# A hybrid convolution and attention layer: which converted weights are kept in DRAM, marks per group of values, and the meta tokens' values by head

## The chip, the core and the metric

The kernel runs on one core of a Trainium2 chip. The time is that of one execution on the device, in microseconds (us). Of several executions the median counts. A profile comes from one execution, and its span runs from the first to the last instruction.

The engines named below each take their instructions in order: TensorE (PE) multiplies matrices and transposes, with its weight loads as PEld; VectorE (DVE) and ScalarE (ACT) do arithmetic on what PE leaves in its accumulators and on buffers; GpSimd (POOL) does arithmetic on buffers and starts some transfers from its own DMA queue (q0); SyncE (SP) starts the other transfers (q1). Sixteen DMA engines move the data of both queues.

## What is computed

One layer over 2048 frames of 1024 channels, with 16 learned meta tokens ahead of them. Both halves of the layer read one input projection of the normalized input:

```python
u = rms_norm(h, pre_g)
proj = u @ w_in
glu_a, glu_b, conv_gate, q, k, v, sb_gate = split(proj)      # 7 x 512 columns

c = glu_a * sigmoid(glu_b)
c = causal_depthwise_conv(c, conv_w, conv_b)                  # width 31
c = silu(layer_norm(c, conv_ln_g, conv_ln_b))
c = c @ w_pw2 + b_pw2                                         # second convolution product
c = c * silu(conv_gate)

s = stick_breaking_attention(q, k, v)                         # 8 heads x 64, strictly causal
s = s * silu(sb_gate)

mixed = concatenate([c, s]) @ w_out
h = h + rms_norm(mixed, post_g)                               # the meta tokens are dropped
```

In the stick-breaking attention the weight of key s for query t is beta(t, s) times the product of 1 - beta(t, j) over the keys j between them, with beta = sigmoid(q.k / 8). The kernel forms the running products P with a scan from the last key backwards, and multiplies them with differences of neighbouring values, so that no subtraction of products is needed.

## The kernel before

**Precision.** All is float32. For the matmuls each operand is split into a high part, as PE's fast float32 form holds it, and a low part that is left over; a product is three matmuls: high by high, high by low, low by high. So each weight has to be converted: `split` (L442) has ACT copy the raw slab to the high part (`high`), and POOL, or for the very first slabs DVE, subtract that from the raw slab (`low`).

**Weights.** `slab_keys` (L57) cuts all weights into slabs of 128 x 512. `specs` (L465) lists them in the order in which the products use them: for chunk 0 the gated linear unit (`G_B`, `G_A`), keys, values, queries; and then for each of the four chunks the attention gate (`G_SG`, 8 slabs), the output product of the chunk before (16 slabs), the convolution gate (`G_CG`, 8), the second convolution product (`w_pw2`, 4) and the next chunk's input products (40); in the last chunk its own output product instead of the last. Lines 504 to 521 work through this list and mark each use of a slab: `kept`, if its converted form lies in DRAM (`wscr`) already, or `save`, if it is to be put there after the conversion. Slabs of the first turn (chunk 0's input products) are not saved, and those that are used again later are saved at their next use. So chunk 0's gates, the second convolution product and chunk 1's input products are saved as they are used in chunk 0, and chunk 0's output product in chunk 1. From then on all slabs are fetched.

`prepare` (L538) takes the next slab in that order and gives it a buffer, at the moment when another has been released. There are four buffers named w. Once no raw slab is left to be loaded, the two large buffers wr, in which raw slabs land in pairs, serve as two more. A kept slab is one transfer of 512 KB into its buffer (`w<-wscr` or `wr<-wscr` in the profile). A raw slab is half of a pair of 512 KB (`wr<-wpack`), and is then converted (`w<-wr` on ACT and on POOL); a saved one is also written out by POOL's queue (`wscr<-w`). `load_raw` (L529) brings the next pair when one has been converted.

**Chunks.** The frames are worked in four chunks of 512. `attention(c)` (L1200) goes through the eight heads and the key blocks from the chunk itself back to the first: `weigh` forms scores (tiles T), sigmoid on ACT, and the scan on DVE (pr); `flip` transposes the products on PE and splits them on ACT and DVE (ah, al); `gather` multiplies them with the value differences (vk) into av. Keys, queries and value differences pass through DRAM (kscr, qscr, vscr). Beside it run the other products of the same chunk: `sb_gate`, `out_proj` of the chunk before, `conv_gate`, `conv_out`, and the next chunk's `turn_in` (its input transposed to uh, ul) and `in_proj`. The convolution's 31 taps are done on DVE (cv, acc), or for some channels of chunks 2 and 3 on ACT and POOL (pd, acc). `conv_norm` transposes the sums for the layer norm.

**Order.** The order on each engine is fixed when the program is built. `Clock` and `Engine` (L85, L166) carry an estimate of when each tile is ready and each engine free. `merge` interleaves the attention, the other products and a third stream by it. Work that depends on other engines is put off with `when(what, ins, outs, date=...)`: it is placed as soon as the estimate says that its inputs are ready and its date has come, or when something needs one of its `outs`. An entry in `outs` may be a string, a mark; `force(mark)` places everything at once that is still put off under that mark.

**Values and meta tokens.** `values` (L935) projects the values in four groups of 128 channels (two heads each), takes the differences on POOL, transposes them on PE (`turn`) and stores them to vscr. All four groups of a chunk use one mark, `"v"`, and `load_v` (L1203) forces it before the first load of a chunk's own block. The meta tokens' keys and values have buffers of their own (km, vm). `meta_v` (L1003) is put off by 15 us from the second key block of chunk 0 on and then starts 16 small transfers, two for each head, one behind the other on SP; `meta_keys`, in chunk 1, is the first to read vm.

Of the kernel before, what the change touches and what calls it, by code (L numbers as in the profile page):

```python
# [254 lines left out]
def trunk(ctx: ExitStack, tc: tile.TileContext, x, xturn, meta, cpack, post_g, wpack, out):  # L255
# [25 lines left out]
    def in_us(t, what, ins=(), outs=()):  # L281
        when(what, ins, outs, date=pe.now + t)
# [227 lines left out]
    place = {key: wscr[i] for i, key in enumerate(again)}  # L510
    order = []
    there = set()
    for turn, (w, n0, cols, ka, kb) in specs():
        step_k = 4 * P // cols
        for k0 in range(ka, kb, step_k):
            key = w, n0, cols, k0
            n = (min(k0 + step_k, kb) - k0) * cols
            kept, save = key in there, key not in there and key in place and turn > 0
            if save:
                there.add(key)  # L520
            order.append((key, n, kept, save))
# [413 lines left out]
    def values(c):  # L935
# [3 lines left out]
        for j in range(NJ):  # L939
# [16 lines left out]
            def differences(vt, j):  # L956
                o = 0 if c == 0 else NM
                dv = T("ev", [P, 1 + NM + TC], EV)[:, : NM + TC]
                pool.tensor_tensor(
                    dv[:, o:], vt[:, o : NM + TC], vt[:, o + 1 :], op=ALU.subtract  # L960
                )
                pool.tensor_copy(vcol[c % 2][:, j], vt[:, NM + P :: P])
                when(lambda: turn(dv, j, P, NM, NTB), [dv], ["v"], tag="T")
                if c == 0:
                    when(lambda: turn(dv, j, NM, 0, 1), [dv], ["v"], tag="T")

            def turn(dv, j, rows, t0, nb):
                pt = PT("T", [P, NTB, P])[:rows, :nb]
# [2 lines left out]
                for b in range(0, nb, 2):  # L971
                    n = min(2, nb - b)
                    part = T("mixs", [P, 2, 4, HD], 8, F32R)[:rows, 0:n]
                    hi, lo = part[:, :, 0::3, :], part[:, :, 1:3, :]
                    d = pt[:, b : b + n].rearrange("p b (h d) -> p b h d", d=HD)
                    act.activation(hi, d, AF.Copy)
                    dve.tensor_tensor(lo, d, hi.bitcast(F32), op=ALU.subtract)
                    row = c * TC + t0 + b * rows
                    when(
                        lambda row=row, n=n, part=part: sp.dma_start(  # L980
                            vscr[j, row : row + n * rows, :].rearrange(
                                "(b p) d -> p b d", p=rows
                            ),
                            part.rearrange("p b k d -> p b (k d)").bitcast(F32),
                        ),
                        [part], ["v"],
                    )

            when(lambda vt=vts[0], j=j: differences(vt, j), [vts[0]], [vcol[c % 2], "v"])
            if c == 0 and j == 0:  # L990
                in_us(4.5, meta_k, outs=[km])

# [8 lines left out]
                )  # L1001

    def meta_v():  # L1003
        force("v")
        for h in range(NH):
            e, j = h % 2, h // 2
            rows = slice(e * HD, (e + 1) * HD)
            for i in range(2):
                blk = (0 if i == 0 else 1) if e == 0 else (3 if i == 0 else 2)
                sp.dma_start(  # L1010
                    vm[h * NM : (h + 1) * NM, i, j, rows].bitcast(F32),
                    vscr[j, 0:NM, blk * HD : (blk + 1) * HD],
                )

    def sb_gate(c):
        for j in range(NJ):
# [183 lines left out]
    def attention(c, mixs):  # L1200
        heads = {}

        def load_v(h, kc):  # L1203
            if kc == c:
                force("v")
            s0, e = NM + kc * TC, h % 2
            vk = T("vk", [P, NTB, P], 2, F32R)
            sp.dma_start(
# [214 lines left out]
    def meta_keys(c, h0, h1, mixs):  # L1423
# [4 lines left out]
            given=lambda: all(("total", c, h) in keep for h in range(h1))  # L1428
            and (c < NCH - 1 or ("conv", c) in keep)
        )  # L1430
        force("v")
        bm = ev()[:, :TC].rearrange("p (b h s) -> p b h s", b=NTB, h=NH)
        hold.add(bm.name)
        if part:
# [339 lines left out]
    def tail(c):  # L1774


        force("v")
        sw, gates = [], [T("mixc", [P, TC], 8) for _ in range(NJ)]
        one = [conv_gate(c, gates), conv_out(c, sw, gates, mixc[c])]
        two = [conv_parts(c, accs[c], sw)]  # L1780
# [123 lines left out]
```

## Time and profile before

| | us |
|---|---|
| median of 3 executions | 1346.3 |
| lowest and highest of them | 1344.78 and 1350.51 |
| the profiled execution, by its own time | 1350.23 |
| its span, from the first to the last instruction | 1348.5 |

The page lists the busy time of each engine, the granted clock of PE in forty slices, the DMA queues, the chain of work that ended last, the costliest groups of instructions and the transfers. Nearly all instructions are issued by one helper (L206), so a group is told apart by its tiles: `w<-wr` is the conversion of a weight slab, `wscr<-w` its store. A group's row gives busy us and mean ns of one instruction, and behind the second bar the idle time before these instructions with what ended it. A row of a transfer in the view of DMA issues gives their number, the KB of one, and the median us from issue to landing.

### The profile page before, as it was taken

What the parts mean: (1) busy time and instruction counts of PE and PEld (TensorE: products, weight loads), DVE (VectorE), ACT (ScalarE), POOL (GpSimd) and SP (SyncE); (2) the same over time, 40 slices, a digit from 0 to 9 for tenths busy, and PEclk for the clock granted to TensorE, in tenths of its full rate; (3) what the DMA queues carried; (4) which work ended last, traced back from release to release, by engine and by line L of the source; (5) the groups of instructions that cost most, each with busy time, mean ns of one, the idle gap of its engine ahead of it and who ended that gap; (6) DMA issues with size and microseconds to landing.
All of it is one profiled execution on the core that took longest, in us unless ns stands there. A gap on an engine that the chain in (4) does not pass through costs nothing.

```text
span 1348.5 us, 21801 instructions
## 1 busy us (share of the span) xinstructions
PE 1315.5 (98%) x7582; PEld 1128.2 (84%) x7582; DVE 1014.4 (75%) x1426; ACT 723.5 (54%) x1443; POOL 644.6 (48%) x781
## 2 busy tenths in 40 slices
PE   8999989999999999999999999999999999999997
PEld 8997868887789877887789988888777899988797
DVE  5999875998985467984495478895548989798865
ACT  6443444344446453476644455478775656555542
POOL 3555567667456540487731243199885121141300
PEclk9999989999999999999999999999999999999999
DMA  6376975899977894686766596557677545687645
GB/s 225 131 213 217 311 261 209 274 328 307 352 236 255 286 341 134 203 239 210 263 214 189 186 326 210 165 181 228 212 218 250 160 143 154 186 278 216 200 156 180
DMA packets 163774, 304.96 MB, mean 226 GB/s; under 512 B 16704, under 2 KB 71168, under 8 KB 163664
## 3 DMA queue, kind: packets, MB, share of 16 engines
q1 hardware_dynamic: 149360, 253.49, 60.0%
q0 software_dynamic: 14304, 50.08, 9.5%
q8 instruction: 60, 0.98, 0.3%
q14 instruction: 50, 0.41, 0.1%
HBM read 221.85 MB, written 81.66 MB: 225 GB/s over the span
## 4 chain that ended last, share of the span: by engine, by line
PE 78%; DVE 8%; DMA 5%; ACT 4%; issue 3%; POOL 2%; SPq 1%; DVEq 0%; ACTq 0%; POOLq 0%
PE mm L206 50%; PE T L206 19%; PE av L206 8%; DMA tok<-x 2%; DVE tok L206 2%; DVE cv L206 1%; DVE pr L206 1%; ACT ev L206 1%; DVE al L206 1%; DMA wr<-wpack 1%; DMA ev<-x 1%; DVE ul L206 1%; DMA ev<-post_g 1%; POOL ev L206 1%; SPq L206 1%
## 5 line engine op out<-in xcount | busy, mean ns | idle before, releaser
L206 PE MATMUL mm<-uh,w 128*128 128x512 f32 (+1 forms) x1632 | 508.4, 372 | 0.4 <-ACT uh L206 0.4
L206 PEld LDWEIGHTS mm<-uh,w 128*128 128x128 f32 x1632 | 294.6, 189 | 48.7 <-ACT uh L206 0.8
L206 DVE TENSOR_TENSOR al<-T,ah 128x512 fp32r<-128x512 f32 (+3 forms) x323 | 194.0, 601 | 159.3 <-ACT ah L206 158.0
L206 PE MATMUL mm<-ul,w 128*128 128x512 f32 (+1 forms) x816 | 300.3, 368 | 1.1 <-DVE ul L206 1.1
L206 DVE TENSOR_TENSOR_SCAN pr<-T,pr,zcol 128x512 f32<-128x512 f32 x192 | 245.0, 1276 | 49.7 <-ACT T L206 44.5
L206 ACT ACTIVATE ah<-T 128x512 fp32r<-128x512 f32 (+3 forms) x323 | 171.7, 532 | 151.0 <-PE T L206 149.6
L206 DVE SCALAR_TENSOR_TENSOR cv<-ct,cp,cv 128x512 f32<-128x512 f32 x319 | 239.2, 750 | 7.1
L206 ACT ACTIVATE T<-T 128x512 f32<-128x512 f32 (+2 forms) x320 | 167.5, 525 | 107.2 <-PE T L206 100.6
L206 POOL TENSOR_TENSOR acc<-acc,pd 128x512 f32<-128x512 f32 x150 | 194.4, 1296 | 44.5 <-ACT pd L206 37.5
L206 PE MATMUL T<-kk,q 128*128 128x512 f32 (+2 forms) x640 | 195.4, 388 | 4.3 <-DVE ul L206 2.6
L206 POOL TENSOR_TENSOR w<-wr,w 128x512 fp32r<-128x512 f32 x109 | 141.0, 1295 | 91.1 <-ACT w L206 81.0
L206 PE MATMUL T<-ident,pr 128*128 128x128 f32 x1088 | 172.1, 273 | 1.6 <-DVE al L206 1.0
L206 PEld LDWEIGHTS mm<-ul,w 128*128 128x128 f32 x816 | 154.2, 189 | 21.7 <-DVE ul L206 1.5
L206 PEld LDWEIGHTS T<-ident,pr 128*128 128x128 f32 x1088 | 133.5, 140 | 33.6 <-DVE pr L206 2.4
L206 DVE TENSOR_TENSOR_SCAN pr<-T,tri 128x128 f32<-128x128 f32 (+3 forms) x128 | 103.9, 815 | 26.4 <-ACT T L206 25.6
L206 PEld LDWEIGHTS T<-kk,q 128*128 128x128 f32 x640 | 105.9, 190 | 20.4 <-DVE ul L206 3.8
L206 PE MATMUL av<-ah,vk 128*128 128x512 f32 (+1 forms) x320 | 117.3, 367 | 1.4 <-ACT ev L206 1.4
L206 ACT ACTIVATE w<-wr 128x512 fp32r<-128x512 f32 x116 | 72.6, 628 | 85.3 <-PE mm L206 39.9
L206 PE MATMUL av<-al,vk 128*128 128x512 f32 (+1 forms) x320 | 117.1, 366 | 0.0
L206 ACT ACTIVATE pd<-ct,cp 128x512 f32<-128x512 f32 x150 | 106.0, 717 | 19.0 <-POOL acc L206 18.1
L206 PE MATMUL mm<-uh,wr 128*128 128x512 f32 x320 | 115.0, 402 | 0.0
L206 POOL COPY cm<-pr 128x1 f32<-128x1 f32 x120 | 25.4, 213 | 139.0 <-DVE pr L206 137.7
(190 smaller groups left out, 1816.8 us busy)
## 6 DMA issues: line engine op xcount, KB each, us to landing
w<-wscr SPq DMA_DIRECT2D x128, 512.0 KB, 4.3
wscr<-w POOLq DMA_DIRECT2D x76, 512.0 KB, 5.5
wr<-wscr SPq DMA_DIRECT2D x62, 512.0 KB, 4.2
wr<-wpack SPq DMA_DIRECT2D x57, 512.0 KB, 5.3
kk<-kscr SPq DMA_DIRECT2D x80, 256.0 KB, 5.1
vk<-vscr SPq DMA_DIRECT2D x80, 256.0 KB, 4.0
q<-qscr SPq DMA_DIRECT2D x64, 256.0 KB, 5.7
tok<-x SPq DMA_DIRECT2D x16, 512.0 KB, 7.0
```

What stands on the lines that cost most here:

```text
L206: return call(out, *args, **kw)
```

## The change

It has three parts. The slabs of the two gates and of the second convolution product are no longer saved: `save` now holds only for `w_out` and for the columns of `w_in` that belong to neither gate (`apart` lists the column groups of both gates). So these slabs are loaded raw and converted in each of the four chunks. The mark `"v"` becomes four marks, `"v0"` to `"v3"`, one for each group of values; where all were forced, all four still are, and `load_v` forces only the mark of its own head's group. And `meta_v` no longer starts its 16 transfers one behind the other: it puts off two for each head, with dates 4 us apart.

```diff
--- before.py
+++ after.py
@@ -510,12 +510,15 @@
     place = {key: wscr[i] for i, key in enumerate(again)}
     order = []
     there = set()
+    apart = [g + j for g in (G_SG, G_CG) for j in range(NJ)]
     for turn, (w, n0, cols, ka, kb) in specs():
         step_k = 4 * P // cols
         for k0 in range(ka, kb, step_k):
             key = w, n0, cols, k0
             n = (min(k0 + step_k, kb) - k0) * cols
             kept, save = key in there, key not in there and key in place and turn > 0
+
+            save = save and (w == w_out or w == w_in and n0 // P not in apart)
             if save:
                 there.add(key)
             order.append((key, n, kept, save))
@@ -960,9 +963,9 @@
                     dv[:, o:], vt[:, o : NM + TC], vt[:, o + 1 :], op=ALU.subtract
                 )
                 pool.tensor_copy(vcol[c % 2][:, j], vt[:, NM + P :: P])
-                when(lambda: turn(dv, j, P, NM, NTB), [dv], ["v"], tag="T")
+                when(lambda: turn(dv, j, P, NM, NTB), [dv], [f"v{j}"], tag="T")
                 if c == 0:
-                    when(lambda: turn(dv, j, NM, 0, 1), [dv], ["v"], tag="T")
+                    when(lambda: turn(dv, j, NM, 0, 1), [dv], [f"v{j}"], tag="T")
 
             def turn(dv, j, rows, t0, nb):
                 pt = PT("T", [P, NTB, P])[:rows, :nb]
@@ -983,10 +986,10 @@
                             ),
                             part.rearrange("p b k d -> p b (k d)").bitcast(F32),
                         ),
-                        [part], ["v"],
+                        [part], [f"v{j}"],
                     )
 
-            when(lambda vt=vts[0], j=j: differences(vt, j), [vts[0]], [vcol[c % 2], "v"])
+            when(lambda vt=vts[0], j=j: differences(vt, j), [vts[0]], [vcol[c % 2], f"v{j}"])
             if c == 0 and j == 0:
                 in_us(4.5, meta_k, outs=[km])
 
@@ -1001,16 +1004,21 @@
                 )
 
     def meta_v():
-        force("v")
+        for j in range(NJ):
+            force(f"v{j}")
         for h in range(NH):
-            e, j = h % 2, h // 2
-            rows = slice(e * HD, (e + 1) * HD)
-            for i in range(2):
-                blk = (0 if i == 0 else 1) if e == 0 else (3 if i == 0 else 2)
-                sp.dma_start(
-                    vm[h * NM : (h + 1) * NM, i, j, rows].bitcast(F32),
-                    vscr[j, 0:NM, blk * HD : (blk + 1) * HD],
-                )
+            in_us(4.0 * h, lambda h=h: meta_v_of(h), outs=[vm])
+
+    def meta_v_of(h):
+
+        e, j = h % 2, h // 2
+        rows = slice(e * HD, (e + 1) * HD)
+        for i in range(2):
+            blk = (0 if i == 0 else 1) if e == 0 else (3 if i == 0 else 2)
+            sp.dma_start(
+                vm[h * NM : (h + 1) * NM, i, j, rows].bitcast(F32),
+                vscr[j, 0:NM, blk * HD : (blk + 1) * HD],
+            )
 
     def sb_gate(c):
         for j in range(NJ):
@@ -1202,7 +1210,7 @@
 
         def load_v(h, kc):
             if kc == c:
-                force("v")
+                force(f"v{h // 2}")
             s0, e = NM + kc * TC, h % 2
             vk = T("vk", [P, NTB, P], 2, F32R)
             sp.dma_start(
@@ -1428,7 +1436,8 @@
             given=lambda: all(("total", c, h) in keep for h in range(h1))
             and (c < NCH - 1 or ("conv", c) in keep)
         )
-        force("v")
+        for j in range(NJ):
+            force(f"v{j}")
         bm = ev()[:, :TC].rearrange("p (b h s) -> p b h s", b=NTB, h=NH)
         hold.add(bm.name)
         if part:
@@ -1774,7 +1783,8 @@
     def tail(c):
 
 
-        force("v")
+        for j in range(NJ):
+            force(f"v{j}")
         sw, gates = [], [T("mixc", [P, TC], 8) for _ in range(NJ)]
         one = [conv_gate(c, gates), conv_out(c, sw, gates, mixc[c])]
         two = [conv_parts(c, accs[c], sw)]
```

## The prediction

> **What bounds the kernel now.** I read the page first (busy shares, granted clock), then the stretches of 33.7 us, then the waits of TensorE, and then one place in time at full resolution.
>
> ```profile
> span 1348.5 us, 21801 instructions
> PE 1315.5 (98%) x7582; PEld 1128.2 (84%) x7582; DVE 1014.4 (75%) x1426; ACT 723.5 (54%) x1443; POOL 644.6 (48%) x781
> 0.00:33.70 33.70, 28.91 (x213) 27.69 (x214) 17.42 (x32) 21.45 (x38) 11.88 (x28) 1.00 0.65 225
> 168.50:202.20 33.70, 27.96 (x136) 22.78 (x135) 25.40 (x41) 14.74 (x30) 21.68 (x31) 0.88 0.72 260
> 202.20:235.90 33.70, 33.52 (x153) 27.43 (x153) 17.29 (x26) 16.54 (x31) 25.49 (x30) 0.91 0.60 209
> 1314.30:1348.00 33.70, 25.80 (x198) 24.67 (x195) 18.52 (x39) 9.22 (x31) 3.09 (x4) 0.95 0.52 180
> PE mm L206 <- POOL w L206: 0.5, 1, 0.5
> ```
>
> TensorE (PE) is the bound: it works 1315.5 of 1348.5 us, and the change alters no matmul. What can be won is in the 33 us in which it stands idle, and in the stretches where its granted clock is below 1.00. Of the idle time 4.8 us lie in the first stretch and 7.9 us in the last, where the change does nothing. In between one stretch stands out, 168.5 to 202.2: 5.7 us idle and a mean clock of 0.88, followed by one with 0.91. (A stretch row is: length, then busy us of PE, PEld, DVE, ACT and POOL with their counts, granted clock, DMA share, GB/s.) No wait of PE names a DMA, and weights that came late cost it 0.5 us in all. So the waits behind that dip have to be found engine by engine.
>
> ```profile
> 172.00:176.00 4.00, 2.83 (x18) 2.22 (x17) 3.05 (x5) 0.00 (x0) 0.75 (x2) 1.00 1.05 409
> 176.00:180.00 4.00, 1.85 (x9) 1.51 (x8) 2.23 (x5) 2.50 (x5) 2.38 (x3) 0.66 0.34 128
> 180.00:184.00 4.00, 4.00 (x14) 3.41 (x13) 2.76 (x6) 0.00 (x0) 3.48 (x9) 0.50 0.66 252
> 196.00:200.00 4.00, 2.25 (x18) 1.91 (x17) 3.30 (x5) 3.61 (x7) 3.46 (x5) 1.00 1.01 370
> 200.00:204.00 4.00, 3.15 (x15) 2.29 (x13) 3.65 (x6) 3.46 (x8) 2.56 (x4) 0.64 0.88 294
> 204.00:208.00 4.00, 4.00 (x15) 3.31 (x14) 2.45 (x4) 0.78 (x2) 2.03 (x3) 0.50 0.11 41
> 175.21 0.33 PE L206 MATMUL T<-ident,acc 128*128 128x128 f32 x1 [1.17 <-DVE acc L206]
> 176.58 0.63 ACT L206 ACTIVATE w<-wr 128x512 fp32r<-128x512 f32 x1 [7.88 <-DMA wr<-wpack]
> 177.12 0.58 ACT L206 ACTIVATE ah<-T 128x512 fp32r<-128x512 f32 x1
> 178.48 1.12 PE L206 MATMUL T<-ident,acc 128*128 128x128 f32 x4 [2.15 <-DVE al L206]
> 199.54 0.51 PE L206 MATMUL T<-kk,q 128*128 128x256 f32 x2 [1.75 <-DVE ul L206]
> ```
>
> There are two stalls. In the **first**, ACT takes its instructions in order, and the conversion of a raw weight slab (w<-wr) waits 7.88 us for its load. Behind it stands the copy ah, behind that DVE's al, and PE waits 2.15 us for al. Just before, PE waited 1.17 us for the last convolution tap (acc), which is a matter of DVE. After the two the clock falls to 0.50. In the **second**, at 199.54, nothing waits for a load: ACT is busy 3.61 and 3.46 of 4 us, and ul comes after uh in its queue.
>
> Why was that load late?
>
> ```profile
> q1 hardware_dynamic: 1323, 2.21, 53.3%
> q0 software_dynamic: 684, 2.53, 48.3%
> wscr<-w POOLq DMA_DIRECT2D x4, 512.0 KB, 7.7
> wr<-wpack SPq DMA_DIRECT2D x2, 512.0 KB, 9.3
> wr<-wpack SPq DMA_DIRECT2D x57, 512.0 KB, 5.3
> ```
>
> The first four rows are the DMA view of 164 to 177 us, the last is the same view of the whole run. In those 13 us the two queues together fill the 16 engines (53.3 + 48.3%). All of q0's 2.53 MB are stores from POOL's queue, which here are wscr<-w: the converted slabs of the gates being saved. The raw loads took 9.3 us to land where 5.3 is their median.
>
> By the Trainium skill, "DMA: Bandwidth & Descriptors", section "Queues, rings and completion order", each DMA engine serves the rows that have work in turn, a packet at a time. By that rule the load gets its share back once the stores are gone; if the load were late by itself, the gain below would be 0. The two shares of about one half each speak for the rule.
>
> **The change, part by part.**
>
> ```profile
> w<-wscr SPq DMA_DIRECT2D x128, 512.0 KB, 4.3
> wr<-wscr SPq DMA_DIRECT2D x62, 512.0 KB, 4.2
> L206 POOL TENSOR_TENSOR w<-wr,w 128x512 fp32r<-128x512 f32 x109 | 141.0, 1295 | 91.1 <-ACT w L206 81.0 <-PE T L206 8.2 <-DMA w<-wscr 1.5
> L206 ACT ACTIVATE w<-wr 128x512 fp32r<-128x512 f32 x116 | 72.6, 628 | 85.3 <-PE mm L206 39.9 <-DMA wr<-wpack 23.1 <-POOL cm L206 8.1
> L206 POOL DMA_DIRECT2D wscr<-w x76: 533/563/790, 126.7 to 445.0; - x76
> 165.62 10.86 DMA wr<-wpack
> ACT w L206 <- DMA wr<-wpack: 23.1, 8, 7.9
> ```
>
> *Weights not kept.* A chunk uses 8 slabs of the attention gate, 8 of the convolution gate and 4 of the second convolution product: 20. All 20 were saved in chunk 0 and fetched back in chunks 1 to 3. Now 20 of the 76 saves go (20 x 0.563 = 11.3 us of POOL, 10.5 MB of stores), 60 fetches of 512 KB go (31.5 MB), and 60 raw slabs come in 30 loads of two (15.7 MB): 26 of 305 MB less traffic. Added are 60 conversions, 60 x 0.628 = 37.7 us on ACT, and 60 subtractions, 60 x 1.295 = 77.7 us on POOL.
>
> What the saves give back: they are the first 20 of the 76, from 126.7 us on, and those four of 164 to 177 us are among them. Without them a raw load of 5.3 us in place of 10.9 (the chain's row at 165.62) shortens ACT's wait by about 5.5 us, to 2.4. That is more than the 2.15 us which PE stood, so the second wait of the first stall goes. The 1.17 us before it stay. And the clock?
>
> ```profile
> 488.00:492.00 4.00, 2.57 (x14) 1.82 (x13) 3.15 (x5) 3.64 (x8) 2.77 (x6) 1.00 1.05 386
> ```
>
> A single wait of 1.43 us left the clock at 1.00 here, as 1.17 us alone then should. At half speed PE worked from 178.5 to 184, 5.5 us, which cost 2.75. So the stall costs 1.17 + 2.15 + 2.75 = 6.1 us, and its removable part is 2.15 + 2.75 = **4.9 us**; the bounds are 0 (another instruction at that place is late as well) and 6.1.
>
> By the Trainium skill, "TensorE: Matmul & The Clock Gate", Part 1, the clock halves after an idle window of about 3.4 us. By that rule 1.17 us alone costs no clock and the sum is 4.9; if any wait of over 1 us cost it, only the 2.15 us would be won. The trace agrees with the rule only roughly: here 3.3 us idle within 5 us were enough.
>
> The second stall costs 1.75 + 0.85 us of idle time (the rows from 196 to 204) and about 6.3 us at half speed, 3.1: 5.7 us. Its cause is ACT's queue, from which the change takes nothing. I leave it in, with bounds of 0 and -5.7.
>
> What the conversions cost:
>
> ```profile
> 640.00:702.00 62.00, 61.70 (x316) 49.92 (x316) 41.11 (x62) 35.43 (x64) 37.64 (x42) 1.00 0.76 248
> 1180.00:1257.00 77.00, 76.80 (x407) 63.59 (x406) 69.16 (x88) 43.95 (x87) 23.28 (x32) 1.00 0.79 242
> ```
>
> These are the stages around chunk 2's attention gate and chunk 3's convolution gate, among the fuller ones for ACT. An attention gate adds 8 conversions (5.0 us of ACT, 10.4 of POOL), a convolution gate with its product 12 (7.5 and 15.5). In the first POOL comes to 37.6 + 10.4 and ACT to 35.4 + 5.0 of 62 us, in the second to 23.3 + 15.5 and 44.0 + 7.5 of 77. Both have room, and matmuls of other work cover them: I take 0. The hazard is the one of the first stall: a conversion that waits for its load holds up ACT. In the run of before 8 waits came with 57 full raw loads, one of them reached PE hard. 30 more loads, with less traffic beside them, make half a case: 0 to 6.1 us each, and I take 0 because the nearest rows (the seven other waits) cost nothing.
>
> *Two weight buffers fewer in chunks 1 to 3.* Buffers wr serve as fifth and sixth weight buffer only once no raw slab is left to load (the 62 fetches wr<-wscr). Now that is so only from the end of chunk 3's gates on. Chunk 0's input products and the output product in chunk 1 ran with four already, and PE waited 0.5 us for weights in all: 0, with an upper bound of a few waits of that size, 2 us.
>
> *Marks by group; meta values a head at a time.*
>
> ```profile
> L206 SPq DMA_DIRECT2D vscr<-mixs x12: 359/387/477, 91.6 to 113.4; - x12
> L206 SPq DMA_DIRECT2D vk<-vscr x1: 1064/1064/1064, 138.4 to 138.4; - x1
> 171.10 11.54 SPq L206 DMA_DIRECT2D vm<-vscr  x16
> 182.73 0.40 SPq L206 DMA_DIRECT2D wr<-wpack  x1
> 190.19 0.62 ACT L206 ACTIVATE w<-wr 128x512 fp32r<-128x512 f32 x1
> ```
>
> Chunk 0's values were all stored by 113.4 us, the first load that forces the mark came at 138.4: the finer mark brings nothing. The 16 small loads hold SP's queue for 11.54 us; behind them stood one raw load (182.73), whose conversion at 190.19 shows no wait. Spread out they cost the same 16 issues, two at a time, and nobody waits: 0. Their bound is that raw load, earlier by up to 11.5 us, worth at most a share of the second stall.
>
> **Sum.** 0 - 4.9 + 0 + 0 = -4.9 us. The profiled execution took 1350.23 us (span 1348.5 and 1.7 around it), 3.9 more than the median 1346.3; I take the sum off the median, since the comparison will be of medians: **1341.4 us**. From the profile's own time it would be 1345.3, which stays in my range.
>
> **The rivals.**
>
> *Both stalls go.* For it: the engines are full in the second too (DMA share 1.01 at 196 to 200), and earlier raw loads may take the crowding off ACT. Against it: no DMA is named in the second. 1341.4 - 5.7 = 1335.7, and some of the smaller waits may go too, down to 1331.
>
> *Nothing comes of it*, or it is given back: the saves go but ACT waits for DVE's last tap or for another load, or one of the 30 new loads makes one stall like the first. 1346.3, or 1341.4 + 6.1 = 1347.5.
>
> *Slower:* the raw loads of chunk 1's gate land in another full stretch.
>
> ```profile
> 484.00:488.00 4.00, 4.00 (x20) 3.21 (x19) 1.08 (x2) 1.79 (x4) 0.54 (x1) 1.00 1.03 411
> 504.00:508.00 4.00, 3.35 (x16) 2.26 (x16) 4.00 (x6) 2.94 (x6) 1.47 (x2) 1.00 1.06 259
> ```
>
> Around 484 the DMA engines are full (residuals and results of chunk 0), and after 500 PE already waits a little, at clock 1.00. A fetch from wscr there holds up only its matmul; a raw slab holds up ACT, and so all of attention. It decides from about 2 us of extra wait, when the clock falls as well: 6.1 us a time. Three such in chunks 1 and 2 give 1341.4 + 18.3 = 1359.7. Against it: the traffic there shrinks too, and two pairs are loaded well ahead.
>
> **How the numbers follow.** Forecast 0.38 (own range 1337 to 1345.5), both stalls 0.27, nothing or given back 0.20, slower 0.15. 0.5% is 6.7 us, about what a measurement of this kernel can tell from no change; below 1339.6 lie the second case and 0.11 of the first: faster 0.38. Slower 0.15, same 0.47. The range 1331 to 1353 holds all but the slower case and the lowest 0.03.
>
> **What would show it.** Right: between 165 and 185 us no wait of ACT for wr<-wpack over 3 us, the clock at 1.00 there, 56 saves in place of 76, 60 fetches fewer and 30 raw loads more, PE's busy time unchanged. The second dip near 200 still there says forecast, gone says the first rival. Wrong: a clock below 1.00 in chunks 1 to 3 behind ACT waits for wr<-wpack (the slower rival), or a dip in chunk 0 with the same length behind another releaser.

## The result, and the profile after

The changed kernel takes 1353.28 us in the median of 13 runs (1351.79 to 1356.67), the kernel before 1346.83 in 13 runs beside it: ratio **1.0052** [1.0038, 1.0066], some 6.5 us longer, where 4.9 us shorter was forecast. The profiled execution took 1356.45 us, 3.2 above that median.

First the page of the changed kernel, in the order of the rows of before: span, busy time by engine, POOL's DMA queue.

```profile
span 1354.5 us, 21858 instructions
PE 1315.9 (97%) x7582; PEld 1128.1 (83%) x7582; DVE 1024.7 (76%) x1426; ACT 753.2 (56%) x1503; POOL 713.0 (53%) x821
q0 software_dynamic: 11424, 39.59, 7.7%
```

TensorE does the same work (1315.9 for 1315.5 us). POOL and ACT are 68.4 and 29.7 us busier (66.4 and 37.7 had been worked out). DVE, which got no new instruction, is busy 10.3 us longer.

The same stretches as before follow (length, then busy us of PE, PEld, DVE, ACT and POOL with counts, granted clock, DMA share, GB/s), with ACT's wait for raw weights.

```profile
168.50:202.20 33.70, 31.58 (x172) 26.28 (x171) 27.93 (x46) 19.47 (x40) 20.64 (x27) 0.95 0.34 100
202.20:235.90 33.70, 33.70 (x158) 27.55 (x157) 18.15 (x28) 15.78 (x30) 26.16 (x32) 1.00 0.73 241
640.00:702.00 62.00, 60.69 (x312) 48.90 (x311) 44.07 (x64) 37.00 (x68) 45.04 (x47) 1.00 0.66 206
1180.00:1257.00 77.00, 74.97 (x391) 61.38 (x390) 70.54 (x84) 46.82 (x91) 34.03 (x41) 1.00 0.66 206
ACT w L206 <- DMA wr<-wpack: 21.5, 13, 3.2
```

Chunk 0 did what was forecast: ACT's longest wait for a raw slab is 3.2 us instead of 7.9, the clock is 0.95 and 1.00 instead of 0.88 and 0.91. The counts came out too: 56 saves, 87 full raw loads for 57, 130 full fetches for 190. But in the two stages that had been costed at nothing TensorE now stands 1.31 us of 62 and 2.03 of 77, against 0.30 and 0.20 before. And the rest is where nobody looked: behind the last matmul. These are the rows of the kernel's last line, an engine's closing instruction (DRAIN: minimum, median and longest in ns, first and last start), first of before, then of after.

```profile
L1900 POOLq DRAIN  x3: 40/102/2014, 1342.5 to 1348.2; - x3
L1900 SPq DRAIN  x3: 7/7/7, 1347.6 to 1347.9; - x3
```
```profile
L1910 POOLq DRAIN  x3: 40/93/10097, 1343.6 to 1354.2; - x3
L1910 SPq DRAIN  x3: 7/7/7, 1348.7 to 1354.0; - x3
```

POOL's first DRAIN takes 2.01 us before and is over at 1344.5, ahead of the outputs, for which SP waits until 1347.6. After, it takes **10.10 us**, from 1343.6 to 1353.7, while SP is through with the outputs at 1348.7 (its first DRAIN): for 5 us the whole core waits for POOL.

For a budget I gave each matmul a fixed pace (the 30th percentile, over all traces, of the time from its start to the next start, by its form; 1282.4 us in all) and added up what TensorE loses against that pace at equal work. With the 1282.4 us the parts add up to the span (the first includes 1.8 us ahead of the first matmul); work 225 lies behind the stalls of chunk 0, work 1200 behind the last gate. Repeat is a second trace of the kernel before (below).

```
us                     lost to   225 to   1200 to      last matmul   span
                       work 225  1200     last matmul  to the end
before                   26.5     25.5      5.5           8.6       1348.5
before, repeat           21.8     28.2      5.3           8.6       1346.2
after                    18.7     34.5      5.5          13.5       1354.5
```

Against the repeat, whose 1348.02 us lie nearer to the median: 3.1 us won in chunk 0, **6.3 us lost** at the gates of chunks 1 to 3, **4.9 us lost** behind the last matmul, 0.2 elsewhere: 8.3 us of span. These are single traces, and the medians differ by less, 6.5 us. The second column of the table at the end of the experiments tells how far a trace can be trusted: five traces without added conversions (both of before, before_110, before_190, vm_only) have 24.1 to 28.6 us in it, four with 60 of them on POOL (after, w_only, after_130, raw_save) 32.1 to 34.5.

### The profile page after: what moved, and what is told of

The parts are those of the page before. It is cut to its first block, busy times and chain, and to the rows that moved or that the text cites. A ratio compares the mean times of both kernels' runs of the same rounds, so it can differ in the third digit from the quotient of the medians.

```text
span 1354.5 us, 21858 instructions
## 1 busy us (share of the span) xinstructions
PE 1315.9 (97%) x7582; PEld 1128.1 (83%) x7582; DVE 1024.7 (76%) x1426; ACT 753.2 (56%) x1503; POOL 713.0 (53%) x821
## 3 DMA queue, kind: packets, MB, share of 16 engines
q0 software_dynamic: 11424, 39.59, 7.7%
## 4 chain that ended last, share of the span: by engine, by line
PE 77%; DVE 9%; ACT 3%; DMA 3%; issue 3%; POOL 3%; SPq 1%; DVEq 0%; ACTq 0%; POOLq 0%
PE mm L206 48%; PE T L206 20%; PE av L206 8%; DVE cv L206 2%; DVE tok L206 2%; DVE pr L206 1%; DMA wr<-wpack 1%; ACT ev L206 1%; POOL w L206 1%; DVE al L206 1%; DMA tok<-x 1%; DVE ul L206 1%; DMA ev<-post_g 1%; ACT uh L206 1%; DVE sgm L206 1%
## 5 line engine op out<-in xcount | busy, mean ns | idle before, releaser
L206 PE MATMUL mm<-uh,w 128*128 128x512 f32 (+1 forms) x1952 | 624.4, 378 | 0.8 <-ACT uh L206 0.8
L206 PEld LDWEIGHTS mm<-uh,w 128*128 128x128 f32 x1952 | 355.9, 190 | 61.3 <-ACT uh L206 1.2
L206 PE MATMUL mm<-ul,w 128*128 128x512 f32 (+1 forms) x976 | 364.4, 373 | 0.2 <-DVE ul L206 0.2
L206 POOL TENSOR_TENSOR w<-wr,w 128x512 fp32r<-128x512 f32 x169 | 221.8, 1315 | 116.8 <-ACT w L206 111.8
L206 PEld LDWEIGHTS mm<-ul,w 128*128 128x128 f32 x976 | 185.1, 190 | 26.4 <-DVE ul L206 0.8
L206 ACT ACTIVATE w<-wr 128x512 fp32r<-128x512 f32 x176 | 110.1, 628 | 96.3 <-PE mm L206 51.2
L206 PE MATMUL mm<-w,mixc 128*128 128x256 f32 x648 | 87.7, 284 | 0.2 <-ACT tok L206 0.2
L206 PE MATMUL mm<-w,mixs 128*128 128x256 f32 x630 | 86.2, 285 | 1.8 <-POOL w L206 1.7
```

The source lines that it names most:

```text
L206: return call(out, *args, **kw)
```

## The experiments

Three questions: does the end hang on POOL's transfers, what costs TensorE time at the gates, and did the first stall belong to the kernel before at all? Theory: end and gates are two separate costs, the first from the 20 saves that went, the second from conversions on POOL beside DVE. Rival: the conversions alone make both. The spans and DRAIN times of all runs stand in one table at the end of this section. Of each edit only the telling lines are printed.

**The two halves of the change.** *w_only* has the weights' part alone, *vm_only* the marks and the spread meta loads alone.

```diff
 vm_only, against after:
-            save = save and (w == w_out or w == w_in and n0 // P not in apart)
```

> The kernel before with the weights' part of the change alone: gates and second convolution product raw in every chunk, one mark, meta tokens' values in one burst. If the loss comes from the weights (POOL beside DVE, ACT's queue, or the two buffers fewer): ratio 1.004 to 1.007 as after, DVE's busy time some 10 us above the 1014.4 of before. If it comes from the order that the marks and the spread loads give: 1.000 and less, since the saves in chunk 0 are gone.

> The kernel before with the marks and the spread meta loads alone, all gates saved in chunk 0 and fetched as before. If the loss comes from the weights: 0.999 to 1.001, DVE busy near 1014. If from the order: 1.004 or more.

Measured: w_only 1.0056 [1.0036, 1.0077], vm_only 0.9988 [0.9973, 1.0003]. The weights' part has the whole loss, the long DRAIN included; the marks and the meta loads change the time by nothing that can be told from nothing. In the budget they do show in one place: at work 550 to 600 TensorE loses 2.2 or 2.3 us in the five kernels without them (the traces of before, before_110, before_190 and w_only) and 0.8 in the others (late_save 1.5), about 1.5 us won, the size of vm_only's 0.9988.

**The subtractions on DVE** (*dve_sub*) and **the saves a chunk later** (*late_save*). In the first, `redo` holds the 60 uses of these slabs after each one's first.

```diff
 dve_sub:
-                    dve if len(todo_w) in FIRST else pool,
+                    dve if len(todo_w) in FIRST or len(order) - len(todo_w) - 1 in redo else pool,
 late_save:
-            save = save and (w == w_out or w == w_in and n0 // P not in apart)
+            save = save and (turn > 1 or w == w_out or w == w_in and n0 // P not in apart)
```

> The kernel after, with the 60 added subtractions of the gates' slabs in chunks 1 to 3 on DVE in place of POOL. Theory POOL beside DVE (POOL's two-input subtractions make DVE's instructions with two buffers as inputs longer, and PE waits for these): the mean of tok<-tok,st,ev goes back from about 1280 ns to the 1031 of before or less, and the loss goes down although DVE gets 60 x 0.69 = 41 us more work: ratio 0.998 to 1.003. Theory ACT's queue (the 60 conversions on ACT are the cost): nothing gained, 1.005 or more.

> The kernel after, but the 20 gate and product slabs are saved at their use in chunk 1 and fetched in chunks 2 and 3: 20 added conversions in place of 60, and the 20 saves moved from chunk 0 to chunk 1. If each added conversion costs (POOL beside DVE, or ACT's queue): the losses at the gates of chunks 2 and 3 go, those in chunk 1 stay; with the 8 us won in chunk 0 the profile is shorter than that of after by about 5 us, ratio 0.997 to 1.002. If the loss is not tied to the conversions of chunks 2 and 3: 1.004 or more.

Measured: dve_sub 1.0027 [1.0016, 1.0038]: with the same conversions on another engine TensorE loses 28.8 us at the gates instead of 34.5; the DRAIN stays at 10.10. The two groups of DVE's instructions that the theory names are below their length before (1031 and 896 ns):

```profile
L206 DVE SCALAR_TENSOR_TENSOR tok<-tok,st,ev 128x512 f32<-128x512 f32 x24 | 21.1, 895 | 0.0
L206 DVE TENSOR_TENSOR tok<-tok 128x512 f32<-128x512 f32 x12 | 9.2, 763 | 0.4
```

late_save 1.0071 [1.0049, 1.0092]: its DRAIN is short, but it loses 41.3 us between 225 and 1200, most of it near 480 us, where the saves meet a stretch that is full already:

```profile
471.80:505.50 33.70, 29.44 (x137) 23.87 (x137) 22.52 (x31) 17.07 (x33) 23.97 (x33) 0.95 0.96 365
```

So the DRAIN doesn't follow the conversions: short with 20 of them, long with 60 on POOL and with 60 on DVE. It did follow the number of transfers that POOL issues: 110 where it was long, 130 where it was short.

**The count of transfers.** *pad20* adds 20 small transfers to the changed kernel's POOL queue in chunk 3, *after_130* adds 20 one-row ones behind saves between 272 and 339 us, *before_190* adds 60 to the kernel before, and *before_110* takes 20 from it by issuing output stores from SP.

```diff
 pad20 (20 times, in chunk 3):
+                    in_us(40.0 + 2.0 * i, lambda i=i: pool.dma_start(padscr[i], zcol))
 after_130, before_190 (behind saves):
+                                pool.dma_start(padscr[m], both[0:1, 0, :P].bitcast(F32))
 before_110:
-                lambda: pool.dma_start(out[t0 : t0 + P, i * 512 : i * 512 + 512], o), [o]
+                lambda: store_out(out[t0 : t0 + P, i * 512 : i * 512 + 512], o), [o]
+        (sp if len(stores) < 20 else pool).dma_start(dst, src)
```

> The changed kernel with 20 small transfers (512 bytes each, into a scratch tile that nothing reads) issued from POOL's queue in chunk 3, so that POOL issues 130 transfers as the kernel before does, not 110. Theory A (the long last instruction of POOL hangs on how many transfers its queue has issued): the last POOL instruction takes about 2.0 us instead of 10.1, the span ends about 5 us earlier, near 1349.5 us, ratio near 1.0015. Theory B (it hangs on the re-conversions, or on the bytes written): still 10.1 us, span near 1354.5, ratio near 1.005. Under both, TensorE's losses at the six gate places stay.

> The changed kernel with 20 one-row transfers of 512 bytes added to POOL's queue in chunk 1, each right behind one of the saves that are left (into a scratch tile that nothing reads): 130 transfers of POOL, as in the kernel before, with almost no bytes. So far the last POOL instruction took 10.10, 10.75 and 11.08 us at 110, 118 and 122 transfers, which is 1.11 + 0.0817 us for each, and 2.01 at 130. Theory A (the transfers count, and start again from 0 somewhere between 122 and 130): 2.0 us here, span about 5.2 us shorter than the changed kernel's, near 1349, ratio about 1.0015, and what is left is the loss at the gate places less the gain in chunk 0. Theory B (bytes or packets count, which these hardly add to): 10 us, ratio 1.005.

> The kernel before with 60 one-row transfers of 512 bytes added to POOL's queue behind 30 of the saves of chunk 1: 190 transfers, no re-conversions. Theory A1 (the count starts again at 128): 62 transfers past it, 1.11 + 62 x 0.0817 = 6.2 us for the last POOL instruction, span 1 to 2 us longer at the end than with 2.0. Theory A2 (above some count the instruction is short): 2.0 us. Theory B (the re-conversions make it long): 2.0 us. It also gives a second trace of the kernel before up to chunk 1: if the first stall (172 to 184 us, 6.6 us of TensorE) belongs to every execution it is here again; if it comes and goes, it may be absent, and the median of the kernel before carries only a part of it.

> The kernel before with 20 of its 24 output stores of POOL's queue issued from SP's: 110 transfers of POOL, no other part of the change. If POOL's transfers decide (the last instruction is about 1.9 us at 2 past 128, 6.75 at 62 past it and 10.10 at 110), it takes 10.1 us and the kernel before loses what the changed kernel lost: about 5 us, ratio 1.003 to 1.004. If the conversions had a part in it, 2.0 us and ratio 1.000. Chunks 0 to 2 as before, the first stall with or without its 6 us.

pad20's DRAIN came down to 2.01 us as theory A had it, but the kernel took 1.0193 [1.0168, 1.0217]: TensorE waited 18.9 us in three waits for loads kk<-kscr near the added transfers, which are 128 rows of 4 bytes each and took 10 us to land. The other three have no such stall. Their DRAIN rows, of after_130, before_190 and before_110 in turn:

```profile
L1921 POOLq DRAIN  x3: 40/102/1854, 1343.4 to 1349.0; - x3
```
```profile
L1911 POOLq DRAIN  x3: 40/93/6752, 1340.2 to 1347.5; - x3
```
```profile
L1906 POOLq DRAIN  x3: 40/93/10099, 1335.5 to 1346.1; - x3
```

Twenty transfers of 512 bytes, issued from 272 to 339 us, shorten an instruction a thousand us later by 8.2 us, and the changed kernel goes from 1.0052 to **1.0006** [0.9990, 1.0023]. Twenty transfers fewer on POOL's queue, with nothing else of the change, make the kernel before's DRAIN 10.10 us and its time **1.0027** [1.0007, 1.0046] (its runs spread from 1346.72 to 1357.47). before_190 at 1.0002 [0.9987, 1.0017] shows that it isn't a matter of many or few: 6.75 us at 190, where theory A1 had 6.2. Bytes and packets don't decide it: after and after_130 moved 39.59 and 39.60 MB on this queue, with 10.10 and 1.85 us, and 12064 packets in after_130 lie between 11424 in after and 12704 in before_110, which both have 10.10.

**Saves without their use** (*raw_save*): as after, but chunk 0's 20 saves (`gate` in the edit) are stored and never read.

```diff
-            if save:
+            if save and gate:
+                if key in stored:
+                    save = False
+                stored.add(key)
+            elif save:
                 there.add(key)
```

> The changed kernel, which loads the gates' and the second product's weights raw in every chunk, but with the 20 saves of chunk 0 still stored to DRAM and never read: 130 transfers of POOL's queue, 76 saves, 60 conversions more than before. If the saves are what makes the first stall (172 to 184 us), it returns here: a wait of ACT for wr<-wpack of 5 to 8 us and up to 6 us of TensorE. The losses at the gate places of chunks 1 to 3 stay, as in the changed kernel, since the conversions are there. Last POOL instruction about 2.0 us by theory A. Ratio: 1.0015 + 0.0045 = about 1.006 if the stall returns, 1.0015 if it doesn't.

Measured 1.0037 [1.0018, 1.0056]. The DRAIN is short and the gates lose 33.9 us, as expected; the first stall did **not** return. In 164 to 177 us the crowd is the one of the kernel before, yet TensorE lost only 0.7 us in that place:

```profile
q0 software_dynamic: 690, 2.50, 47.8%
q1 hardware_dynamic: 1179, 2.09, 46.7%
wr<-wpack SPq DMA_DIRECT2D x2, 512.0 KB, 7.8
```

Why it is 0.0031 above after_130, at the same count and nearly the same losses in its trace, is open; its runs spread from 1348.83 to 1357.06.

**The kernel before once more** (*before_2*, nothing edited).

> The kernel before once more, for a second trace. If the first stall is the kernel's own, TensorE loses about 6.6 us again between 172 and 184 us, and the time is near 1350; if it comes and goes, it loses 1 to 2 us there, the time is near the median of 1347, and the prediction took 4.9 us off a median that carries only a part of them. Last POOL instruction 2.01 us.

It took 1348.02 us. Its rows for the two stalls (each 12 us long) and for ACT's waits:

```profile
172.00:184.00 12.00, 12.00 (x71) 10.16 (x70) 8.57 (x16) 4.10 (x8) 7.93 (x15) 1.00 0.69 248
196.00:208.00 12.00, 11.35 (x53) 9.26 (x51) 9.00 (x13) 8.07 (x17) 5.73 (x7) 0.72 0.41 131
ACT w L206 <- DMA wr<-wpack: 18.2, 8, 5.3
```

The first stall is absent: 12.00 of 12 us at full clock, though the two raw loads took 7.9 us to land and ACT waited 4.33 us there. Up to that point before_190 and before_110 are the kernel before as well, and lost 1.3 and 2.0 us in place of 6.6. Of four traces one has the stall. The second is in all four (6.8 to 7.0 us at equal work).

**One gate at a time.** *sg_raw* has only the attention gate raw, *cg_raw* only the convolution gate and the second product; *sg_130* is sg_raw with 8 one-row transfers.

```diff
 sg_raw:
-    apart = [g + j for g in (G_SG, G_CG) for j in range(NJ)]
+    apart = [g + j for g in (G_SG,) for j in range(NJ)]
-            save = save and (w == w_out or w == w_in and n0 // P not in apart)
+            save = save and (w != w_in or n0 // P not in apart)
 cg_raw:
+    apart = [g + j for g in (G_CG,) for j in range(NJ)]
```

> Only the attention gate's weights are loaded raw in chunks 1 to 3; the convolution gate's and the second product's are saved as before (68 saves; 122 transfers of POOL's queue). If the re-conversions cost TensorE time where they run, losses appear near 350, 670 and 1030 us and not at the convolution gate's places (440 to 500, 810, 1190): about 5 us of the changed kernel's 11 to 13. First stall: 12 of 20 saves are still there, so between 0 and 6 us. The last POOL instruction tells where the count decides: 2.0 or 10.1 at 122. Ratio 0.999 to 1.004.

> The counterpart: only the convolution gate's and the second product's weights are loaded raw in chunks 1 to 3, the attention gate's are saved as before (64 saves; 118 transfers of POOL's queue). Losses near 440 to 500, 810 and 1190 us and none near 350, 670 and 1030: about 7 us of the changed kernel's. First stall: 8 of 20 saves are still there. Last POOL instruction 2.0 or 10.1 at 118. Ratio 1.000 to 1.005. If the losses of sg_raw and of this one together are well below those of the changed kernel, the saves in chunk 0 matter to both and the parts aren't independent.

> Only the attention gate's weights raw (12 saves of 20 left), with 8 one-row transfers added to POOL's queue: 130. By theory A the last POOL instruction takes 2.0 us, not 11.1, the span ends 6.1 us earlier than that kernel's 1348.5, near 1342.4, ratio 1.0029 - 0.0046 = 0.998: a version as fast as the kernel before or slightly faster. By theory B ratio 1.003.

Measured: 1.0029 [1.0014, 1.0045], 1.0025 [1.0012, 1.0038] and 0.9988 [0.9974, 1.0003]. TensorE's losses appear at each one's own places and not at the other's: near work 1150 cg_raw loses 2.7 us as the changed kernel does, sg_raw 0.6 as the kernel before; near 650 it is 1.3 and 2.6. The sums don't add up, though: between 225 and 1200 sg_raw loses 26.6 us and cg_raw 27.3, 2.5 and 3.2 more than vm_only's 24.1, which has the same marks, while the changed kernel loses 10.4 more. Whether the two gates are not independent or single traces are too coarse for it stays open. Eight short transfers brought sg_130's DRAIN from 11.08 to 1.91 us.

**What a conversion on POOL does to DVE.** The costliest groups on DVE, of before, of its repeat and of after (count, busy us, mean ns):

```profile
L206 DVE SCALAR_TENSOR_TENSOR tok<-tok,st,ev 128x512 f32<-128x512 f32 x24 | 24.5, 1031 | 7.4 <-DMA ev<-x 3.8 <-POOL mixs L206 3.6
L206 DVE TENSOR_TENSOR tok<-tok 128x512 f32<-128x512 f32 x12 | 10.8, 896 | 0.4
```
```profile
L206 DVE SCALAR_TENSOR_TENSOR tok<-tok,st,ev 128x512 f32<-128x512 f32 x24 | 22.8, 956 | 6.9 <-DMA ev<-x 6.9
```
```profile
L206 DVE SCALAR_TENSOR_TENSOR tok<-tok,st,ev 128x512 f32<-128x512 f32 x24 | 30.6, 1283 | 3.0 <-DMA ev<-x 2.9
L206 DVE TENSOR_TENSOR tok<-tok 128x512 f32<-128x512 f32 x12 | 14.4, 1201 | 0.4
L206 POOL TENSOR_TENSOR w<-wr,w 128x512 fp32r<-128x512 f32 x169 | 221.8, 1315 | 116.8 <-ACT w L206 111.8 <-PE T L206 4.0
```

The same instructions on tiles of the same size got 24% to 34% longer. The timeline of after in chunk 3's convolution gate shows how:

```profile
1182.86 1.28 POOL L206 TENSOR_TENSOR w<-wr,w 128x512 fp32r<-128x512 f32 x1
1184.11 1.28 POOL L206 TENSOR_TENSOR tok<-tok,ev 128x512 f32<-128x512 f32 x1
1185.36 1.29 POOL L206 TENSOR_TENSOR mixs<-acc,mixs 128x512 fp32r<-128x512 f32 x1
1186.75 3.79 POOL L206 TENSOR_TENSOR mixs<-acc,mixs 128x512 fp32r<-128x512 f32 x3
1187.84 3.26 DVE L206 SCALAR_TENSOR_TENSOR tok<-tok,st,ev 128x512 f32<-128x512 f32 x1
1191.76 0.66 PE L206 MATMUL T<-ident,pr 128*128 128x128 f32 x4 [1.06 <-DVE al L206]
1195.74 0.73 PE L206 MATMUL T<-kk,q 128*128 128x512 f32 x2 [0.68 <-DVE pr L206]
```

DVE's instruction, 0.72 us at its shortest, starts 0.2 us ahead of the end of one POOL instruction, and two more follow it without a gap: 0.20 + 1.28 + 1.29 us under POOL, then half a microsecond of its own, 3.26 in all. So here it reads as held until POOL pauses, not as slowed. The added conversion stands first in these lines (w<-wr,w); what was behind it on POOL then runs back to back, without a pause. DVE's next two-input work and then PE come late. By the Trainium skill, "SBUF — State Buffer", section "SBUF: two separate sides", VectorE and GpSimd take a shared pair of ports for a whole instruction, and a VectorE instruction with two SBUF inputs then waits for a GpSimd one that reads SBUF. The trace agrees: 3.26 us here, 0.72 alone.

The same hold is in the kernel before, at this place and elsewhere (first line; its longest is 4.28 us at 785.40), and an added conversion can also hold DVE itself (the other two, of after):

```profile
1189.11 2.04 DVE L206 SCALAR_TENSOR_TENSOR tok<-tok,st,ev 128x512 f32<-128x512 f32 x1
```
```profile
1199.56 1.29 POOL L206 TENSOR_TENSOR w<-wr,w 128x512 fp32r<-128x512 f32 x1 [0.94 <-ACT w L206]
1200.01 1.38 DVE L206 SCALAR_TENSOR_TENSOR tok<-tok,st,ev 128x512 f32<-128x512 f32 x1
```

What grew is the number of cases. Of the 36 instructions in the two groups, 8 and 9 took over 1 us in the two traces of before, 22 or 23 in after, w_only, after_130 and raw_save, 7 and 8 in dve_sub and dve_130. In all traces together 191 of the 648 ran with no POOL instruction beside them, and none of these took more than 0.76 us.

*one_in* puts two one-input copies in place of each added subtraction; the low halves of the gates' weights are left out of the computation.

```diff
-            eng.tensor_tensor(lo, y, hi.bitcast(F32), op=ALU.subtract)
+                eng.tensor_copy(lo, y)
+                eng.tensor_copy(lo, hi.bitcast(F32))
```

> The changed kernel in which the 60 added conversions of chunks 1 to 3 have two one-input copies on POOL in place of the one two-input subtraction (the low halves of those slabs are not what the reference's numbers need; the products run as before). POOL is busy about as long or longer beside DVE. If a two-input POOL operation is what slows DVE's two-input operations, DVE's rows come back: tok<-tok,st,ev near 7.6 us over its shortest in all instead of 13.6, and TensorE's losses at the gate places fall by half or more. If any POOL work does it, or the wait for POOL's slab itself, they stay or grow. Last POOL instruction 10.10 us in both cases (110 transfers), ratio 1.002 to 1.004 in the first, 1.005 or more in the second.

```profile
L206 POOL CAST w<-w 128x512 fp32r<-128x512 f32 x60 | 40.6, 676 | 5.4 <-ACT w L206 1.7
L206 POOL CAST w<-wr 128x512 fp32r<-128x512 f32 x60 | 38.6, 644 | 11.2 <-PE mm L206 8.1 <-DMA wr<-wpack 2.6 <-DMA q<-qscr 0.3
L206 DVE SCALAR_TENSOR_TENSOR tok<-tok,st,ev 128x512 f32<-128x512 f32 x24 | 22.1, 928 | 0.5 <-DMA ev<-x 0.4
L206 DVE TENSOR_TENSOR tok<-tok 128x512 f32<-128x512 f32 x12 | 13.2, 1104 | 0.4
```

POOL is busy as long for them (40.6 + 38.6 us for 60 x 1.3 = 78), in pieces of half the length. The first DVE group is back to 928 ns, the second only a third of the way, and the gates lose 31.4 us in place of 34.5; 8.8 of these are one new stall at work 750 to 800, where the changed kernel loses 2.3; the rest is 22.6 in place of 32.2. The ratio, 1.0043 [1.0029, 1.0057], lies between the two cases. A one-input copy holds DVE too, for its shorter time; here one stands alone beside DVE's instruction:

```profile
1203.70 1.17 DVE L206 SCALAR_TENSOR_TENSOR tok<-tok,st,ev 128x512 f32<-128x512 f32 x1
1203.71 0.62 POOL L206 CAST w<-w 128x512 fp32r<-128x512 f32 x1 [0.60 <-ACT w L206]
```

So shorter pieces on POOL hold DVE less, and it isn't the second input of POOL's instruction that makes the hold.

**The conversions off POOL, with a short DRAIN.** *dve_130* is dve_sub with 20 one-row transfers; *cgd_130* is cg_raw with its 36 subtractions on DVE and 12 one-row transfers. The edits are those above.

> The changed kernel with its 60 added subtractions on DVE and 20 one-row transfers more on POOL's queue (130). With POOL's they took 110 transfers, 10.1 us and 1.0027; with a last POOL instruction of 2.0 us the span is 5.1 us shorter, near 1343.3, ratio 1.0027 - 0.0038 = 0.999. If the conversions on POOL are what the rest of the changed kernel's loss is, this beats the changed kernel with 130 transfers (1.0006) by 0.0015 or more; if not, it is the same as that one.

> Only the convolution gate's and the second product's weights are raw in chunks 1 to 3, with their 36 added subtractions on DVE, the attention gate's saved as before, and 12 one-row transfers on POOL's queue (130). The attention gate's places cost what they cost before, the convolution gate's about 1 us less in chunks 1 and 2 and 2 us more in chunk 3, and the end of chunk 3 about 1.4 us less; the first stall is mostly gone (8 saves of 20 left). Last POOL instruction 2.0 us. Span 1341 to 1344, ratio 0.996 to 0.999. Were the conversions harmless on POOL, it would be no better than sg_130's 0.9988.

dve_130: 1344.85 us, **0.9978** [0.9967, 0.9989]. cgd_130: 1337.07 us, **0.9920** [0.9903, 0.9936], 10 us better than the kernel before and more than was expected. It loses 21.4 us at the gates; its windows of 471.8, 640 and 1180 us:

```profile
471.80:505.50 33.70, 32.02 (x171) 26.39 (x170) 28.81 (x39) 22.06 (x43) 13.63 (x20) 1.00 0.75 259
640.00:702.00 62.00, 61.16 (x325) 50.27 (x324) 47.58 (x72) 33.51 (x62) 30.23 (x35) 1.00 0.77 249
1180.00:1257.00 77.00, 76.30 (x416) 63.11 (x415) 74.17 (x101) 46.81 (x92) 22.83 (x32) 1.00 0.71 225
```

The first of them in the repeat of before:

```profile
471.80:505.50 33.70, 31.28 (x155) 24.76 (x154) 23.84 (x32) 18.52 (x36) 13.50 (x22) 1.00 0.91 322
```

There the DMA engines were 0.91 busy, and TensorE lost 6.3 us at work 450 to 500; here it is 0.75 and 2.8 us. That the lighter traffic is the reason is not shown: in the same window sg_raw has 0.81 and loses 6.1 us at that work, and cg_raw, which loads the same slabs as cgd_130 and subtracts on POOL, has 0.89 and loses 5.6. Only the three kernels that have this gate raw and subtract on DVE lose 2.0 to 2.9 there (dve_sub, dve_130, cgd_130). Why the two together do it stays open. So the idea of the change has a worth, for one of its two gates and with the subtraction on the other engine: cg_raw, the same on POOL, loses 27.3 us. The span and the parts of all runs:

```
             transfers  POOL's     225 to  last matmul  span    ratio
             of POOL    DRAIN us   1200    to the end
before          130       2.01      25.5      8.6      1348.5
before_2        130       2.01      28.2      8.6      1346.2
before_110      110      10.10      24.1     13.5      1346.4   1.0027
before_190      190       6.75      28.6     10.2      1347.7   1.0002
vm_only         130       2.01      24.1      8.6      1343.2   0.9988
after           110      10.10      34.5     13.5      1354.5   1.0052
w_only          110      10.10      32.1     13.5      1352.2   1.0056
after_130       130       1.85      34.0      8.5      1349.3   1.0006
raw_save        130       2.01      33.9      9.6      1349.7   1.0037
late_save       130       2.01      41.3      8.3      1355.2   1.0071
pad20           130       2.01      59.8      8.5      1373.8   1.0193
one_in          110      10.10      31.4     13.5      1350.7   1.0043
dve_sub         110      10.10      28.8     13.5      1348.4   1.0027
dve_130         130       1.85      28.2      8.5      1342.0   0.9978
sg_raw          122      11.08      26.6     14.5      1348.5   1.0029
sg_130          130       1.91      28.1      8.8      1344.8   0.9988
cg_raw          118      10.75      27.3     14.2      1350.0   1.0025
cgd_130         130       1.85      21.4      8.3      1336.3   0.9920
```

## Why the prediction was wrong, by its own steps

- **"In the last [stretch], where the change does nothing": this step failed.** The 20 saves were costed at 11.3 us of POOL and at what they do to other transfers. Their number also sets POOL's closing instruction: 2.01 us became 10.10, worth 4.9 us of span. after_130 (1.0052 to 1.0006) and before_110 (1.0027) show it from both sides. No row of before could have given the price; that POOL's DRAIN ended only 3.1 us ahead of the last wait for the outputs could have been read.
- **Conversions, "I take 0": this step failed too.** The hazard that was priced, ACT held by a raw load, did not come (longest wait 3.2 us in 13). The busy time "has room" on POOL, 45.0 of 62 us, was right and beside the point: POOL without pauses holds DVE, and DVE feeds attention. The term measured 6.3 us against the repeat. dve_sub and dve_130 show that most of it is the place of the subtraction: 28.8 and 28.2 us in place of 34.5 and 34.0, where the kernels without added conversions have 24.1 to 28.6. What is left to ACT's conversions and the two buffers is within that spread. one_in supports the hold, with a new stall in it.
- **First stall, -4.9.** It went, and chunk 0 came out as drawn. But the sum was taken off the median, and the stall is in one of four traces of the kernel before up to that point. Against the other three the change wins 2.6 to 3.1 us in chunk 0, most of it in the second stall. "These saves make the load late" holds as far as the crowd goes; that the crowd makes the stall doesn't: raw_save and before_2 have the crowd and not the stall. What else it takes is open.
- **Second stall, left in at 5.7:** it stayed, as forecast, but got smaller: 4.8 us at equal work in after, 6.8 to 7.0 before. "From which the change takes nothing" is too strong: w_only, the weights' part alone, has 4.7 as well. How that part does it isn't settled (vm_only 5.9, raw_save 4.9, sg_130 6.4).
- **Two buffers fewer, marks, meta loads, 0:** vm_only's interval holds 1, though by the budget the marks and the meta loads win about 1.5 us at work 550 to 600. The buffers weren't tried alone; PE's wait for POOL's w is one of 1.7 us, against two that sum to 1.9 in the repeat.
- **Slower rival, 1359.7:** the right side by another mechanism. Chunk 1 near 480 us was the right place to worry about, and late_save shows what a crowd there costs; but it was DVE and POOL, not ACT and a load, that held the changed kernel up.

## What to carry to other kernels

Read the span's end as a stage of its own: which engine's closing instruction is last, and by how much, and count what a change takes from or adds to that engine's DMA queue. When work goes to POOL, its share of busy time says nothing of whether DVE can run beside it: look for DVE's two-input instructions there, and for the pauses that POOL has left. And before a stall is priced, see whether a second trace of the same kernel has it.

## What the runs showed of the hardware

POOL's closing DRAIN depends on how many transfers its queue issued in the whole run, and hardly on what they carry: 10.10, 10.75 and 11.08 us at 110, 118 and 122 (0.082 us for each one more, whichever kernel issued them), 1.85 to 2.01 at 130 (the lower values where 12 or 20 of them have one row), 6.75 at 190. Somewhere between 122 and 130 it begins anew, and from 130 to 190 it grows by 0.079 to 0.082 us each. Where exactly it does, and why, wasn't tried. On the line of the first three values 2.01 and 6.75 us would be the lengths for 11 and 69 transfers, so it doesn't simply start again from nothing behind 122.

A DVE instruction with two buffers as inputs that takes 0.72 us alone took 3.26 beside three POOL instructions in a row. And twenty stores of 128 rows of 4 bytes in chunk 3 came with 25 us more lost by TensorE, 18.9 us of it standing in three waits for loads, where twenty of one row of 512 bytes in chunk 1 cost nothing that shows.
